# First products on x^T as loaded, normalised afterwards, in a hybrid short-convolution / RG-LRU layer

## The chip, the cores and the metric

The kernel runs on one core of one Trainium2 chip. The metric is device time in microseconds (us) of one execution. Names of engines in the profile: PE is TensorE (matmuls; PEld its weight loads), DVE is VectorE, ACT is ScalarE, POOL is GpSimd, SP is SyncE, which only issues DMAs.

## The reference

A decoder layer on x of 2048 positions by 1024 features, in float32. `DEPTH` is 1.

```python
xn = rms_norm(h, ln_g)                              # x / sqrt(mean(x^2) + eps) * ln_g
proj = jnp.einsum('bsd,de->bse', xn, w_in)          # 1024 -> 6 x 1024 columns
b_gate, c_gate, x_conv, g_conv, x_lru, g_lru = jnp.split(proj, splits, axis=-1)
y_conv = b_gate * causal_conv3(c_gate * x_conv)
y_conv = headwise_rms_norm(y_conv, 8, conv_out_g) * silu(g_conv)
u = causal_conv4(x_lru) + conv_b                    # then r, i from block-diagonal maps of u
a = exp(8 * r * log_sigmoid(lam)); drive = sqrt(1 - a^2) * (i * u)
h_t = a_t * h_{t-1} + drive_t                       # the scan
y_lru = headwise_rms_norm(h_t, 16, lru_out_g) * silu(g_lru)
out = rms_norm(h + concat(y_conv, y_lru) @ w_out, final_g)
```

The first line is what the change is about. The norm multiplies row s of x by one number, its root. In x^T (features on partitions, positions along the free axis) that is a factor for each column, and so it is in every product of a weight block with x^T: one can multiply first and scale the result's columns later.

## The kernel before, in words

**Products.** All arithmetic is on numbers of float32 width. A factor is split in two parts that TensorE takes (`fp32r`): a high part, made by a copy that rounds (`hi`, on ScalarE), and the rest (`low`, line 170, a subtraction on VectorE or POOL). A product of two split tiles is three matmuls of 128x128 by 128x512: high x high, high x low, low x high (`mm`, line 1023; "product" in this document means one such matmul). Tiles `th`/`tl` hold the parts of x^T (set `T[i, j]`, j of 4), `s` those of weights.

**Steps.** The positions are worked on in two halves of 1024, each in two blocks of 512. One step of the table `steps` (line 268) takes two groups of 128 output columns and both blocks of positions; the kinds are "l" (recurrent unit: its input and its gate), "a" and "b" (the convolution's C and x columns; B and gate). The features are halved too, so a step works on 2x2 blocks of weights and of x^T. From the fourth step on it uses a scheme of 7 block products (with sums of blocks, `s_plan`, line 192) in place of 8. The first three steps are plain: 96 products each, in four banks of PSUM called 11, 12, 21, 22: first digit the column group, second the block of positions. `prep` makes the next step's weight tiles while a step runs.

**Order of the work.** Each engine takes its instructions in the order in which the program writes them (`manual_schedule`, line 1067); nothing reorders them. Work after a bank is done is put off with `at(n, ...)`, line 144: it is written at the n-th `tick()` from there, and a tick comes ahead of every half bank of products in a plain step (line 1227). So the consumers `lru` (line 720), `conv_a` (834) and `conv_b` (870) write their parts among later steps: for "l" the bank copies, four convolution taps, tiles `st` (the split of u), the gate matmuls (line 764), sigmoids, tanh, exponential, root, scan. A gate matmul in TensorE's queue holds up all products behind it until its `st` tile is there.

**The opening.** SyncE loads the first four blocks of x as rows (512 KB each), weights of the first two steps and the next four blocks of x. `norm_rows` (line 527) squares a block on ScalarE, and VectorE scales it. `turn` (line 563) transposes four blocks to one x^T tile on TensorE (4 transposes of 128x128), and ScalarE or VectorE evicts it times `ln_g`. `first(j)` does that for the first block of 512 positions and `second(j)` for the second. `spin` writes transposes of the identity, which nobody reads, into TensorE's queue. The first step multiplies the first 512 positions (banks 11, 21), then the others (12, 22). The second step ("a") runs whole after it; `after1`/`after2` write the third step's weight split and the sums of x^T blocks (`bit`, line 1195) among the products.

## Time and profile before

| | |
|---|---|
| median of 3 runs | 1300.43 us (1299.43 to 1300.56) |
| the profiled execution | 1301.88 us, of which the span is 1300.0 us |
| granted TensorE clock | 0.998 |
| PE busy | 1284.9 us (99%) |
| DVE busy | 1030.9 us (79%) |
| ACT busy | 748.0 us (58%) |
| POOL busy | 207.2 us (16%) |
| DMA | 355.27 MB, mean 273 GB/s |

The page and the views behind it are of one execution. A row of a timeline gives the start in us from the span's begin, the duration, the engine, the line of the kernel, the operation, output and input tiles, sizes, how many instructions were merged, and in brackets the idle time ahead of it and what ended that. A line can be a helper's: L163 is every addition, subtraction and multiplication of two tensors. Where instructions follow each other closely, the start of the next is a better price than the duration, since durations of neighbours overlap by some 0.1 us.

### The profile page before, as it was taken

The numbers are of one execution on the slowest core, as the hardware profiler recorded it, in microseconds if no ns is written. First come the engines' busy times: TensorE is split into PE (matmuls) and PEld (weight loads), VectorE is DVE, ScalarE is ACT, GpSimd is POOL, SyncE is SP. The second block draws the span as 40 slices with busy tenths as digits, with TensorE's granted clock in tenths as the row PEclk, the third lists the DMA queues.
The fourth block names the chain that finished last, engine by engine and source line by source line (L and its number), as shares of the span: only waits on it lengthen the run. The fifth ranks groups of instructions, "written<-read, shape, count | busy, mean of one in ns | idle before, by whom it ended". The sixth has DMA issues, their size and how long they took to land.

```text
span 1300.0 us, 16684 instructions
## 1 busy us (share of the span) xinstructions
PE 1284.9 (99%) x5688; PEld 1059.0 (81%) x5688; DVE 1030.9 (79%) x1303; ACT 748.0 (58%) x1143; POOL 207.2 (16%) x173
## 2 busy tenths in 40 slices
PE   8999999999999999999999999999999999999997
PEld 6878888888888888888887888888888888887886
DVE  7799898999999988968656765677559777659886
ACT  8586857667565757666463636455466433445453
POOL 3102323332432320010010120101011000000000
PEclk9999999999999999999999999999999999999999
DMA  7138887898988888552899999999789897697654
GB/s 297 33 130 307 289 310 272 295 342 296 326 307 311 306 289 308 187 182 65 282 348 281 330 357 321 336 350 369 229 269 335 253 263 243 245 403 287 236 188 152
DMA packets 157956, 355.27 MB, mean 273 GB/s; under 512 B 16944, under 2 KB 51760, under 8 KB 157872
## 3 DMA queue, kind: packets, MB, share of 16 engines
q1 hardware_dynamic: 153264, 338.17, 75.6%
q0 software_dynamic: 4320, 15.73, 3.1%
q8 instruction: 45, 0.74, 0.2%
q10 hardware_dynamic: 288, 0.32, 0.1%
q14 instruction: 39, 0.32, 0.1%
HBM read 217.11 MB, written 137.04 MB: 272 GB/s over the span
## 4 chain that ended last, share of the span: by engine, by line
PE 88%; DVE 5%; DMA 4%; issue 1%; ACT 1%; POOL 0%; SPq 0%; DVEq 0%; POOLq 0%
PE bank L1028 86%; PE gate L764 2%; DVE s L163 1%; DMA s<-sd 1%; DMA tl<-td 1%; DMA xr<-od 1%; DMA s<-so 1%; DVE ob L163 0%; DVE raw L163 0%; DMA zr<-rsd 0%; DMA yd<-gl 0%; DVE tl L163 0%; ACT th L261 0%; POOL tl L163 0%; DVE x L551 0%
## 5 line engine op out<-in xcount | busy, mean ns | idle before, releaser
L1028 PE MATMUL bank<-th,s 128*128 128x512 f32 x3616 | 1121.7, 389 | 2.0 <-DMA s<-sd 0.7
L1028 PEld LDWEIGHTS bank<-th,s 128*128 128x128 f32 x3616 | 678.7, 188 | 145.5 <-ACT q L1364 1.9
L1028 PE MATMUL bank<-tl,s 128*128 128x512 f32 x1808 | 704.3, 390 | 0.5 <-POOL tl L163 0.2
L1028 PEld LDWEIGHTS bank<-tl,s 128*128 128x128 f32 x1808 | 339.4, 188 | 72.5 <-POOL tl L163 1.1
L163 POOL TENSOR_TENSOR s<-raw,s 128x512 fp32r<-128x512 f32 x62 | 114.0, 1852 | 283.9 <-ACT s L213 224.5
L213 ACT CAST s<-raw 128x512 fp32r<-128x512 f32 x140 | 84.5, 618 | 32.9 <-PE bank L1028 19.1
L163 DVE TENSOR_TENSOR s<-raw,s 128x512 fp32r<-128x512 f32 (+1 forms) x125 | 84.9, 702 | 10.2 <-ACT s L1091 6.5
L163 DVE TENSOR_TENSOR tl<-traw,th 128x512 fp32r<-128x512 f32 x85 | 58.3, 719 | 19.9 <-ACT th L451 10.0
L163 DVE TENSOR_TENSOR s<-s,s 128x512 fp32r<-128x512 f32 x105 | 73.0, 695 | 1.1 <-ACT s L213 1.1
L213 ACT CAST s<-s 128x512 fp32r<-128x512 f32 x105 | 65.0, 619 | 10.4 <-DVE s L163 10.4
L163 POOL TENSOR_TENSOR gb<-gb,sg 128x1024 f32<-128x1024 f32 x8 | 21.7, 2715 | 296.9 <-ACT sg L695 259.2
L736 DVE SCALAR_TENSOR_TENSOR u<-xl,pt,u 128x1024 f32<-128x1024 f32 x48 | 61.6, 1283 | 6.8 <-ACT u L732 6.2
L1364 ACT COPY q<-bank 128x512 f32<-128x512 f32 x58 | 33.8, 583 | 49.6 <-PE bank L1028 45.6
L848 DVE SCALAR_TENSOR_TENSOR t<-p,pt,t 128x1024 f32<-128x1024 f32 x32 | 46.5, 1453 | 15.0 <-ACT t L845 14.3
L163 DVE TENSOR_TENSOR st<-u,st 64x512 fp32r<-64x512 f32 x64 | 52.4, 818 | 2.0
L771 ACT ACTIVATE r<-gate,pt 64x512 f32<-64x512 f32 x64 | 43.7, 684 | 17.2 <-PE gate L764 16.4
L163 DVE TENSOR_TENSOR raw<-raw,zr 128x512 f32<-128x512 f32 x64 | 41.1, 682 | 8.7 <-DMA zr<-rsd 8.7
L1368 ACT COPY rr<-bank 128x512 f32<-128x512 f32 x31 | 18.1, 584 | 49.4 <-PE bank L1028 49.4
L771 ACT ACTIVATE i<-gate,pt 64x512 f32<-64x512 f32 x64 | 43.8, 684 | 1.1
L451 ACT CAST th<-traw 128x512 fp32r<-128x512 f32 x64 | 36.2, 618 | 13.3 <-DVE traw L163 10.7
L163 DVE TENSOR_TENSOR traw<-traw 128x512 f32<-128x512 f32 x60 | 41.7, 699 | 2.7 <-DMA traw<-in_w_out_dram 1.7
L1368 ACT COPY u<-bank 128x512 f32<-128x512 f32 x27 | 15.8, 585 | 47.7 <-PE bank L1028 47.1
(181 smaller groups left out, 1272.4 us busy)
## 6 DMA issues: line engine op xcount, KB each, us to landing
sd<-s SPq DMA_DIRECT2D x151, 512.0 KB
s<-sd SPq DMA_DIRECT2D x151, 512.0 KB
raw<-in_w_in_dram SPq DMA_DIRECT2D x104, 256.0 KB
raw<-yd SPq DMA_DIRECT2D x64, 256.0 KB
traw<-in_w_out_dram SPq DMA_DIRECT2D x64, 256.0 KB
so<-so SPq DMA_DIRECT2D x22, 512.0 KB
s<-so SPq DMA_DIRECT2D x22, 512.0 KB
yd<-gl SPq DMA_DIRECT2D x32, 256.0 KB
```

The costliest lines, as they stand in the source:

```text
L163: (eng or nc.vector).tensor_tensor(out=out, in0=a, in1=b, op=op)
L213: nc.scalar.copy(dst[i][0], val(i))
L451: nc.scalar.copy(self.dst[i, j][0], self.r[i, j])
L736: nc.vector.scalar_tensor_tensor(out=v["u"], in0=o1[:, 1 + j:1 + j + N2], scalar=lw[j], in1=v["u"], op0=ALU.mult, op1=ALU.add)
L764: nc.tensor.matmul(ps[j], v["gw"][n][:, j, :], v["st"][j][:, sl], start=(n == 0), stop=(n == 1))
L771: nc.scalar.activation(out=g_[hi, sl], in_=v["ps"][j][src], func=AF.Sigmoid, bias=pt[src, bias + k:bias + k + 1])
L848: nc.vector.scalar_tensor_tensor(out=tcur["t"], in0=p[:, 2 + j:2 + j + N2], scalar=cw[j], in1=tcur["t"], op0=ALU.mult, op1=ALU.add)
L1028: nc.tensor.matmul(bank, a[:, js], b, start=start and n == 0, stop=stop and n == 2, skip_group_check=more)
L1364: nc.scalar.copy(q1, bk["A"])
L1368: nc.scalar.copy(u2, bk["A"])
```

## The change: what it does

- x^T is loaded from a copy of x in DRAM that is stored by columns (`in_xt`, used before for later positions only): eight blocks of 128 features by 512 positions. They are scaled by `ln_g` and split (`raw_hi`, `raw_lo`), not normalised. `first` and its 32 transposes fall away.
- TensorE runs banks 11 and 21 of step one on them and then banks 11 and 21 of step two (`products`). Four banks hold raw results. Banks of step one are copied out (`RAW`), and one of step two; the other is read where it lies.
- The first 512 rows of x are loaded a second time as half rows (`xh`), squared on ScalarE and VectorE, summed, and rooted: one number per position. `roots` transposes it, spread over 128 columns, so that a tile `rr` has the roots along the free axis, the same on all partitions.
- The raw results are multiplied by `rr`. x^T, still in SBUF, is multiplied by `ln_g` and `rr` in one instruction per block (`scaled`, eight of them on VectorE), and split anew, eight casts on ScalarE and eight subtractions on POOL, for the third step and the sums.
- `second`, banks 12 and 22 of step one and then of step two follow. Step two has four ticks behind that point in place of eight, so what is put off by ticks moves: the first gate matmuls stand behind 228 products, where they stood behind 192. The sums of blocks (`bit`) are written two a tick. `klam` (a small constant) is made later. The recurrent unit's result of the first pair goes into tile `u`, not into `gl`.

The order on three engines. TensorE's first instructions (`tp` is a transpose's output, `x_152` to `x_155` the first four blocks of x). Before:

```order
L561 MATMUL spin<-ident 128x128 x28
L567 MATMUL tp<-ident,x_152 128x128
L561 MATMUL spin<-ident 128x128 x4
L567 MATMUL tp<-ident,x_153 128x128
L561 MATMUL spin<-ident 128x128 x4
L567 MATMUL tp<-ident,x_154 128x128
```

Now:

```order
L541 MATMUL spin<-ident 128x128 x34
L1152 MATMUL bank<-th,s 128x512 x4
L1152 MATMUL bank<-tl,s 128x512 x2
L1152 MATMUL bank<-th,s 128x512
L1152 MATMUL bank<-tl,s 128x512
```

The products come directly behind the spins; no transpose stands ahead of them. VectorE, at the last turned block of `second` and behind it (`rr` is the spread roots, `xl` and `gl` the copies of step one's raw banks). Before:

```order
L574 TENSOR_SCALAR traw<-tp,pt 128x512
L163 TENSOR_TENSOR tl<-traw,th 128x512
L163 TENSOR_TENSOR s<-raw,s 128x512 x2
L580 MEMSET rs_659 128x32
L163 TENSOR_TENSOR traw<-traw 128x512 x2
L736 SCALAR_TENSOR_TENSOR u<-xl,pt,u 128x1024 x2
```

Now:

```order
L552 TENSOR_SCALAR traw<-tp,pt 128x512
L162 TENSOR_TENSOR tl<-traw,th 128x512
L162 TENSOR_TENSOR xl<-xl,rr 128x512
L162 TENSOR_TENSOR gl<-gl,rr 128x512
L1207 SCALAR_TENSOR_TENSOR traw<-traw,pt,rr 128x512 x8
L558 MEMSET rs_704 128x32
L162 TENSOR_TENSOR traw<-traw 128x512 x2
L162 TENSOR_TENSOR s<-raw,s 128x512
L716 SCALAR_TENSOR_TENSOR u<-xl,pt,u 128x1024 x2
```

Ten instructions, two scalings of copies and eight of x^T, now stand ahead of the sums and the taps. POOL from its first weight split on. Before:

```order
L163 TENSOR_TENSOR s<-raw,s 128x512 x2
L163 TENSOR_TENSOR tl<-traw,th 128x512 x7
L724 MEMSET xl 128x4
L838 MEMSET p 128x2
L711 TENSOR_SCALAR bh<-bd 128x256
```

Now:

```order
L162 TENSOR_TENSOR s<-raw,s 128x512 x2
L162 TENSOR_TENSOR tl<-raw,th 128x512
L704 MEMSET xl 128x4
L162 TENSOR_TENSOR tl<-traw,th 128x512 x12
L825 MEMSET p 128x2
L691 TENSOR_SCALAR bh<-bd 128x256
```

Of the twelve low parts of x^T four are `second`'s and eight those of the scaled blocks; all twelve stand behind the opening.

The core of the diff:

```diff
-        for b in range(NB - 2):
-            norm_rows(b)()
...
+        def get_x(kt):
+            nc.sync.dma_start(tr[kt % NB][kt // NB * 2], xt[kt * P:(kt + 1) * P, 0:C])
...
+        for f, *v in ((get_w, 0, 0), (get_x, 0), (get_w, 0, 2), (get_x, 1), (get_x, 2), (get_x, 3),
+                      (get_w, 0, 1), (get_x, 4), (get_w, 0, 3), (get_x, 5), (get_x, 6), (get_x, 7),
+                      (get_w, 1, 0), (get_w, 1, 2), (get_w, 1, 1), (get_w, 1, 3)):
+            f(*v)
         for b in range(NB, 2 * NB):
             nc.sync.dma_start(x0[b], x[b * P:(b + 1) * P, :])
...
+        for b in range(NB):
+            for n in range(2):
+                nc.sync.dma_start(xh[b][n], x[b * P:(b + 1) * P, n * C:(n + 1) * C])
...
+        def raw_hi(kt, eng=None):
...
+                nc.scalar.activation(out=T[i, j][0], in_=tr[j][i // 2], func=AF.Copy, scale=gain(kt))
...
+        def raw_lo(kt):
+            i, j = kt // NB * 4, kt % NB
+            nc.vector.scalar_tensor_tensor(out=T[i, j][1], in0=tr[j][i // 2], scalar=gain(kt),
+                                           in1=T[i, j][0].bitcast(F32), op0=ALU.mult, op1=ALU.subtract)
...
+        raw = [[bank(), bank()] for _ in range(2)]
+        for part in range(2):
+            for j in range(NB):
+                products(0, raw[0], part, j, (0, 4), j == 0)
+        for b in range(NB, 2 * NB):
+            norm_rows(b)
+        lru0 = lru(0, 0)
+        lru0(11, raw[0][0], RAW)
+        lru0(21, raw[0][1], RAW)
...
+        for part in range(2):
+            for j in range(NB):
+                if part == 1 and j == 2:
+                    second(0)
+                products(1, raw[1], part, j, (0, 4))
...
+        tt(rs0, rs0, rest, ALU.add)
+        nc.scalar.activation(out=rs0, in_=rs0, func=AF.Sqrt, scale=1.0 / D, bias=eps)
+        nc.vector.reciprocal(out=rs0, in_=rs0)
+        conv0 = conv_a(0, 0)
+        conv0(21, raw[1][1], RAW)
+
+        def roots():
+            ps = pss.tile([P, C], F32, tag="s", name="rsb")
+            for b in range(NB):
+                nc.tensor.transpose(ps[:, b * P:(b + 1) * P], rs0[:, b:b + 1].broadcast_to((P, P)), ident)
+            rsb[0] = sm("rr")
+            nc.scalar.copy(rsb[0], ps)
+
+        def scaled(j):
+            for i in (0, 4):
+                v = tr[j][i // 2]
+                nc.vector.scalar_tensor_tensor(out=v, in0=v, scalar=gain(j + i), in1=rsb[0],
+                                               op0=ALU.mult, op1=ALU.mult)
+                Tp[j].hi(i)
+                Tp[j].lo(i, g)
...
             if j == 2:
...
+                roots()
+                lru0(11, None, rsb[0])
+                lru0(21, None, rsb[0])
+            if j >= 2:
+                scaled(2 * j - 4)
+                scaled(2 * j - 3)
...
+        for which, b in plain(1, (22, 12), after1):
+            kept[which] = b
+        conv0(12, kept[12], None)
+        conv0(21, None, rsb[0])
```

More of the change, by code (lines that the diff above doesn't have):

```diff
@@ L858, in put @@
             else:
-                xx[which] = aux("xx")
+                if which not in xx:
+                    xx[which] = aux("xx")
                 combine(xx[which], bank, other)
+                if other is RAW:
+                    return
             if which == 12:
@@ L1067, in hymba_kernel, with get_w @@
     with tc.manual_schedule(engines={ENG.PE, ENG.Activation, ENG.DVE, ENG.Pool, ENG.SP}):
-        spin(28)
-        make_klam()
-        Wr = [load_s(0)]
+        spin(34)
+        klam_late = make_klam()
+        Wr = [[piece("raw") for _ in range(4)] for _ in range(2)]
+        tr = [{} for _ in range(NB)]
+        raw0 = [wt("hl", "traw", bufs=HL) for _ in range(NB)]
+        for j in range(NB):
+            for i in range(2):
+                tr[j][2 * i] = raw0[j][:, i * C:(i + 1) * C]
+        def get_w(m, i):
+            half, q = divmod(i, 2)
+            nc.sync.dma_start(Wr[m][i], w_in[cols[steps[m][0]][half] + steps[m][2], q])
@@ L1095, in s_lo @@
         def s_lo(m, i, eng=None):
             low(Wr[m][i], Sp[m][i], eng)
-        tr = [{} for _ in range(NB)]
-        Tp = [TPrep(j, tr[j], T) for j in range(NB)]
-        raw0 = [wt("hl", "traw", bufs=HL) for _ in range(NB)]
-        def first(j):
-            for i in range(2):
-                tr[j][2 * i] = raw0[j][:, i * C:(i + 1) * C]
-                turn(0, j + i * NB, tr[j][2 * i], i, 0 if i or j else 4)
-        for i in range(3):
-            s_hi(0, i)
-        s_lo(0, 0, g)
-        s_lo(0, 2, g)
@@ L1112, in hymba_kernel @@
+        s_hi(0, 0, nc.vector)
+        raw_hi(0, nc.vector)
+        s_lo(0, 0)
+        s_hi(0, 2)
+        raw_lo(0)
+        s_lo(0, 2)
+        for kt in range(1, NB):
+            raw_hi(kt)
+            raw_lo(kt)
+        s_hi(0, 1)
         s_lo(0, 1)
-        Tp[0].hi(0)
+        raw_hi(4)
+        raw_lo(4)
         s_hi(0, 3)
-        Tp[0].hi(4)
-        Tp[0].lo(0)
-        s_lo(0, 3)
-        Tp[0].lo(4)
-        c11, c21 = bank(), bank()
-        def spread(order):
-            seen = []
-            for cc, i, w, t, v in order:
-                nc.tensor.matmul(cc, Sp[0][i][w][:, 0:P], T[t, 0][v], start=not any(b is cc for b in seen),
-                                 stop=False)
-                seen.append(cc)
@@ new lines, in hymba_kernel, with products @@
+        for kt in range(NB + 1, 2 * NB):
+            raw_hi(kt)
+            raw_lo(kt)
+        for i in (0, 2, 1, 3):
+            s_hi(1, i)
+            s_lo(1, i, g if i > 1 else None)
+        klam_late()
+        def products(m, cc, part, j, ts, spread=False):
+            a, b = ((cc[n], Sp[m][2 * n + part]) for n in range(2))
+            t = T[ts[part], j]
+            order = ((a, 0, 0), (b, 0, 0), (a, 1, 0), (b, 1, 0), (a, 0, 1), (b, 0, 1)) if spread else (
+                (a, 0, 0), (a, 0, 1), (a, 1, 0), (b, 0, 0), (b, 0, 1), (b, 1, 0))
+            for n, ((bk, s), w, v) in enumerate(order):
+                first = part == 0 and j == 0 and (n < 2 if spread else n % 3 == 0)
+                last = part == 1 and j == NB - 1 and n % 3 == 2
+                nc.tensor.matmul(bk, s[w][:, j * P:(j + 1) * P], t[v], start=first, stop=last,
+                                 skip_group_check=True)
```

176 lines of the change are left out of this document (67 added, 109 removed).

## The prediction

> **What bounds the kernel now.** I read the page first, for the engine that is full; then the windows by stage, for where the others are full too; then the timelines of the opening, because the change ends after the third step.
>
> ```profile
> span 1300.0 us, 16684 instructions
> PE 1284.9 (99%) x5688; PEld 1059.0 (81%) x5688; DVE 1030.9 (79%) x1303; ACT 748.0 (58%) x1143; POOL 207.2 (16%) x173
> ```
>
> TensorE sets the end: it is busy for 99%, and each microsecond by which its queue moves forward or back early stays to the last instruction. The profiled execution took 1301.88 us (1.88 outside the span); that is 1.45 above the median of 1300.43, so I work out a difference and put it on the median. The stages (columns: window, its length, then busy time and count of PE, PEld, DVE, ACT, POOL):
>
> ```profile
> 13.27:43.50 30.23, 29.29 (x144) 22.63 (x145) 21.26 (x28) 22.39 (x42) 9.82 (x9) 1.00 0.54 197
> 43.50:65.35 21.85, 21.85 (x99) 18.06 (x97) 17.52 (x25) 12.32 (x18) 1.77 (x3) 1.00 0.07 23
> 65.35:89.00 23.65, 23.65 (x105) 19.27 (x104) 21.51 (x32) 21.00 (x32) 0.10 (x1) 1.00 0.24 86
> 89.00:139.00 50.00, 49.33 (x217) 40.44 (x216) 48.04 (x55) 33.94 (x53) 13.94 (x10) 1.00 0.84 295
> ```
>
> From 89 to 139 us VectorE is busy for 48.0 of 50 us. It is nearly as full as TensorE, so TensorE cannot be brought forward by much unless VectorE is too. Before 65 us VectorE has some 20 us of idle time.
>
> **The opening, before and after.**
>
> ```profile
> 1.56 5.01 PE L561 MATMUL spin<-ident 128*128 128x128 f32 x28 [1.56 <-POOL ident masks.py:199]
> 8.37 0.33 PE L567 MATMUL tp<-ident,x 128*128 128x128 f32 x1 [1.79 <-DVE x L551]
> 13.27 2.24 PE L1124 MATMUL bank<-th,s 128*128 128x512 f32 x7 [0.41 <-ACT th L261]
> 16.68 1.03 PE L567 MATMUL tp<-ident,x 128*128 128x128 f32 x8
> 17.47 0.47 PE L1028 MATMUL bank<-th,s 128*128 128x512 f32 x1
> 65.35 0.39 PE L764 MATMUL gate<-st,bh 128*128 128x512 f32 x1
> 65.58 0.39 PE L764 MATMUL gate<-st,bl 128*128 128x512 f32 x1
> 4.96 1.06 ACT L539 ACTIVATE junk<-x 128x1024 f32<-128x1024 f32 x1 [0.24 <-DMA x<-in_x_dram]
> 10.00:20.00 10.00, 8.70 (x46) 6.31 (x47) 7.03 (x12) 9.34 (x18) 4.41 (x3) 1.00 1.04 399
> ```
>
> Today the first product runs at 13.27, after load, squares, scaling, transposes and split. The first gate matmul runs at 65.35, when the 192 products of two steps are done. A product costs 0.2275 us start to start (65.58 - 65.35), eight transposes 0.79 (17.47 - 16.68).
>
> In the changed kernel the first product needs one weight block, one block of x^T and their splits. The first 512 KB landed at 4.96 and the loads moved 399 GB/s (last column of the last row), so 256 KB blocks land from about 4.3 on, one each 0.65 us (an estimate from these two rows), always ahead of the six products (1.37 us) that each x^T block feeds. The 34 spins, at 5.01/28 = 0.179, end at 7.65, and by then the five VectorE instructions on the first blocks are about done (0.67 each at most, by a row further down). So products run from 7.65 without a wait: 84 of them take 19.1, to 26.75; eight transposes, to 27.55; twelve more products, to 30.3. **Gain so far** against the old order: about 10 us.
>
> Then a chain of short instructions ends last. ScalarE and VectorE need these prices:
>
> ```profile
> 37.80 0.69 ACT L572 ACTIVATE traw<-tp,pt 128x512 f32<-128x512 f32 x1 [0.80 <-PE tp L567]
> 39.07 0.62 ACT L1159 CAST th<-traw 128x512 fp32r<-128x512 f32 x1 [0.58 <-DVE traw L574]
> 9.08 0.62 ACT L536 ACTIVATE junk<-x 128x512 f32<-128x512 f32 x1
> 9.60 0.19 ACT L536 ACTIVATION_READ_ACCUMULATOR junk<-x 128x1 f32 x1
> 34.56 0.74 DVE L574 TENSOR_SCALAR traw<-tp,pt 128x512 f32<-128x512 f32 x1
> ```
>
> Behind the first turned blocks (27.55) ScalarE has an eviction and two casts (to 29.3), then four half-row squares at 0.72 (to 32.1); VectorE has its own four, with a POOL subtraction beside them, to 33.3. Root and reciprocal end at 34.15, and only behind them in VectorE's queue stands the eviction of the second turned block (34.9), then cast (35.5), low part (36.2), POOL's low part (37.45). TensorE waits there with five of twelve products, goes on to 39.3, turns the last block and spreads the roots, to 40.5. The remaining products of both steps, 72 at 0.2275, would end at 56.9 against 65.35: a lead of 8.4 us. The spread roots lie in SBUF at 42.35, after the eviction, two casts and one copy.
>
> **What VectorE must do from 42.35 to the first gate matmul.** By the program the gates now stand behind 228 products, not 192; in the old run that amount of TensorE work is done at 65.35 + 36 x 0.2275 = 73.5. Ahead of the `st` tiles that the gates need, VectorE has: 24 operations of 128x512 on two tensors (two scalings of copied banks, two of kept ones among them), the 8 new L1207 instructions that scale x^T, 3 convolution taps of 1024, one 1024 multiplication and 2 `st` instructions. Their prices, start to start:
>
> ```profile
> 58.36 0.69 DVE L163 TENSOR_TENSOR tl<-traw,th 128x512 fp32r<-128x512 f32 x1
> 58.96 0.69 DVE L163 TENSOR_TENSOR u<-traw 128x512 f32<-128x512 f32 x1
> 252.73 0.74 DVE L604 SCALAR_TENSOR_TENSOR xcol<-xcol,pt 128x512 f32<-128x512 f32 x1
> 253.40 1.28 DVE L848 SCALAR_TENSOR_TENSOR t<-p,pt,t 128x1024 f32<-128x1024 f32 x1
> 47.35 2.60 DVE L736 SCALAR_TENSOR_TENSOR u<-xl,pt,u 128x1024 f32<-128x1024 f32 x2
> 60.77 1.22 DVE L163 TENSOR_TENSOR gl<-gl,sg 128x1024 f32<-128x1024 f32 x1
> 63.35 2.84 DVE L163 TENSOR_TENSOR st<-u,st 64x512 fp32r<-64x512 f32 x4
> ```
>
> 24 x 0.60 + 8 x 0.67 + 3 x 1.22 + 1.13 + 2 x 0.72 = 26.0 us (0.67 is 253.40 - 252.73, the L604 instruction being of the same form). Nothing in that list waits for a product that is done later than that. Alone it would end at 68.4, 5.1 before 73.5.
>
> **The cost that decides: POOL beside VectorE.** The change puts eight POOL subtractions (the low parts of the scaled x^T) beside the eight L1207 and what follows. Here is what such neighbours do today:
>
> ```profile
> 36.55 1.27 POOL L163 TENSOR_TENSOR tl<-traw,th 128x512 fp32r<-128x512 f32 x1 [2.46 <-ACT th L261]
> 37.03 1.34 DVE L163 TENSOR_TENSOR s<-raw,s 128x512 fp32r<-128x512 f32 x1 [0.35 <-ACT s L1091]
> 96.71 1.54 POOL L163 TENSOR_TENSOR s<-raw,s 128x512 fp32r<-128x512 f32 x1 [20.45 <-ACT s L213]
> 97.28 2.06 DVE L677 SCALAR_TENSOR_TENSOR gl<-r,pt,gl 128x1024 f32<-128x1024 f32 x1
> 112.78 3.70 POOL L163 TENSOR_TENSOR s<-raw,s 128x512 fp32r<-128x512 f32 x2 [6.27 <-DMA yd<-gb]
> 111.08 2.56 DVE L736 SCALAR_TENSOR_TENSOR u<-xl,pt,u 128x1024 f32<-128x1024 f32 x2
> 113.55 1.78 DVE L163 TENSOR_TENSOR s<-raw 128x512 f32<-128x512 f32 x1
> 115.37 1.67 DVE L163 TENSOR_TENSOR s<-s,raw 128x512 f32<-128x512 f32 x1
> ```
>
> The VectorE instruction at 37.03 takes 1.34 instead of 0.69 and ends 0.55 after POOL's does: it stood still while POOL worked. The taps at 111.08 ran at full speed although POOL had started at 112.78; POOL waited, and then the two at 113.55 and 115.37 took 3.45 in place of 1.38. The two engines take turns, and where VectorE is full a POOL subtraction costs it (3.45 - 1.38)/2 = 1.04 us. Bounds: nothing (POOL always waits) and POOL's whole 1.27. I take 1.04. Eight cost 8.3, the last subtraction of the third turned block 0.65 (1.34 - 0.69), the gate weights' split about 0.85 (estimate: one subtraction of half the size). Together 9.8.
>
> The first `st` pair is then ready at 42.35 + 26.0 + 9.8 = 78.15, and the gates run 4.7 us later than today, in place of 8.4 earlier. Behind the waiting gates stand all products of the third step. What is late next: ScalarE's copies of weight blocks for that step, which stand behind the eight casts of scaled x^T, so TensorE halts at its start too; these halts lie ahead of the gates and are not added. After the gates VectorE's queue, full until 139, has no more in it than before but for the scan, its copy and the multiplication behind it, 3.6 us that now stand later. The least room there is between the low part that ends at 119.4 and its product:
>
> ```profile
> 92.76 0.50 PE L1028 MATMUL bank<-th,s 128*128 128x512 f32 x1 [0.68 <-ACT q L1364]
> 118.75 0.68 DVE L163 TENSOR_TENSOR s<-s,s 128x512 fp32r<-128x512 f32 x1
> ```
>
> That product runs 132 products after 92.76, near 123; the room of 3.6 us is just used up. I add nothing.
>
> Small parts: 28 transposes fewer are in the times above. The klam instructions move from ahead of the first scaling to where VectorE waits for turned blocks:
>
> ```profile
> 3.25 0.17 DVE L122 TENSOR_SCALAR kl<-kl 128x8 f32<-128x8 f32 x1 [0.27 <-ACT kl L120]
> 7.29 0.17 DVE L138 TENSOR_SCALAR klam<-kl 128x8 f32<-128x8 f32 x1
> ```
>
> Those 4 us are costed at nothing there. SyncE's queue reads 2.1 MB more; at 0.65 us for 256 KB the half rows land by 25, before their squares at 29. If they were late, each microsecond would move the 42.35.
>
> **Sum:** + 4.7 us, so 1301.88 + 4.7 = 1306.6 for an execution like the profiled one, and **1305.2 us** on the median.
>
> **Rivals.**
>
> A, POOL yields. VectorE's queue is back to back, so it may win the turn each time, as the taps at 111.08 did; POOL's low parts are needed only from the third bank of the third step on. The gates are at 68.4 plus the little that is left, and the least room in VectorE's later queue limits the lead to 4 to 5 us: **1296 us**. It decides where a POOL subtraction costs VectorE under (5.1 - 0.65 - 0.85)/8 = 0.45 us. For it: the taps. Against it: the pairs at 37.03, 97.28 and 113.55. The Trainium skill speaks for it in part: "SBUF — State Buffer", section "Who interferes with whom", says that the engine which issues first holds the shared port pair for its whole instruction and that issue order decides who blocks; the rows show both orders, and by turns.
>
> B, VectorE does not matter and the whole lead of 8.4 stays: **1292 us**. Against it: 48.04 busy of 50 us from 89 on.
>
> C, the strided columns of x^T drag the opening loads to half their rate. The half rows then land near 41 and the roots end some 8 us later, and with them all behind: **1313 us**. The weights, in rows of the same 2 KB, were part of the 399 GB/s, so I give it little.
>
> D, the costs meet in the middle (about 0.45 us for each subtraction) and the move does nothing: **1300 us**.
>
> **Chances.** Forecast 0.52 (its own range 1303 to 1308: the subtraction at 1.27, the opening late by 1), A 0.22, B 0.06, C 0.08, D 0.12. A measurement of this kernel can tell 0.2%, 2.6 us. Faster: A and B, 0.28. Within: D and the lower edge of the forecast, 0.14. Slower: 0.58. The range takes in A and ends above the forecast's upper bound: 1295.5 to 1309.5; B and C are left out.
>
> **What would show it.** In the changed profile: first product at about 7.7; L1207 instructions of about 1.7 to 1.9 us each in place of 0.74, with POOL subtractions between them; TensorE idle before the first gate matmuls, released by `st`, which start near 78; VectorE without idle time from 42 to 139. The forecast is wrong if the L1207 take 0.7 (A), if the gates start before 73, or if TensorE's first halves run with gaps that a DMA ends (C).

## The result, and the profile after

The changed kernel takes **1315.78 us** (median of 4, 1314.51 to 1316.63) against 1300.49 of the old one on the same chip: a ratio of 1.0117, 95% interval 1.0099 to 1.0134. It is 15.3 us slower; the forecast was 4.7 slower.

From the page of the profile:

```profile
span 1314.6 us, 16650 instructions
PE 1286.9 (98%) x5654; PEld 1058.6 (81%) x5654; DVE 1045.1 (79%) x1314; ACT 747.6 (57%) x1140; POOL 219.0 (17%) x179
```

The same four stages as before (window, its length, then busy time and count of PE, PEld, DVE, ACT, POOL; then the granted clock):

```profile
13.27:43.50 30.23, 29.36 (x145) 23.90 (x145) 22.24 (x54) 20.23 (x43) 8.49 (x8) 1.00 0.78 302
43.50:65.35 21.85, 17.64 (x76) 13.62 (x74) 21.66 (x21) 12.31 (x19) 13.84 (x9) 1.00 0.00 1
65.35:89.00 23.65, 15.77 (x50) 11.97 (x50) 22.75 (x33) 8.93 (x15) 1.87 (x4) 0.78 0.00 0
89.00:139.00 50.00, 46.03 (x192) 36.53 (x193) 44.74 (x54) 39.48 (x59) 9.77 (x8) 0.97 0.71 251
```

TensorE was busy for all of 43.5 to 89 us in the old kernel; now it is idle for 12 of 45.5 us there, and VectorE is busy for 44.4 of them. From 65 to 89 the granted clock is 0.78 on average. Nearly the whole loss lies ahead of 113 us (13.9 of the 14.6 us between the two profiled spans, worked out below). These are TensorE's halts from 57 us on (its timeline; in brackets the idle time and what ended it); behind the last one it never waits again within 60 us:

```profile
58.88 0.50 PE L1018 MATMUL bank<-th,s 128*128 128x512 f32 x1 [1.51 <-ACT s L1098]
60.48 0.73 PE L1018 MATMUL bank<-th,s 128*128 128x512 f32 x2 [0.87 <-DVE s L162]
66.02 0.94 PE L1018 MATMUL bank<-th,s 128*128 128x512 f32 x2 [2.49 <-DVE s L162]
78.57 0.76 PE L744 MATMUL gate<-st,bh 128*128 128x512 f32 x1 [5.67 <-DVE st L162]
90.11 0.69 PE L744 MATMUL gate<-st,bh 128*128 128x512 f32 x1 [2.67 <-DVE raw L162]
91.52 0.80 PE L744 MATMUL gate<-st,bh 128*128 128x512 f32 x1 [0.28 <-ACT i L751]
105.70 0.50 PE L1018 MATMUL bank<-th,s 128*128 128x512 f32 x1 [1.56 <-ACT q L1399]
112.46 0.50 PE L1018 MATMUL bank<-th,s 128*128 128x512 f32 x1 [1.01 <-ACT rr L1403]
```

Together 16.1 us. In the old kernel there is one halt in that stretch, the 0.68 at 92.76 that the prediction shows. The opening went as forecast: first product at 6.87, the first turned blocks at 26.93, the spread roots in SBUF at 42.86 (forecast 7.65, 26.75, 42.35). VectorE's timeline from there, and ScalarE's copy of the bank that ended the last halt:

```profile
42.86 1.39 DVE L162 TENSOR_TENSOR xl<-xl,rr 128x512 f32<-128x512 f32 x1 [0.32 <-ACT rr L1202]
44.78 10.58 DVE L1207 SCALAR_TENSOR_TENSOR traw<-traw,pt,rr 128x512 f32<-128x512 f32 x8
55.32 3.42 DVE L162 TENSOR_TENSOR traw<-traw 128x512 f32<-128x512 f32 x2
77.74 2.84 DVE L162 TENSOR_TENSOR st<-u,st 64x512 fp32r<-64x512 f32 x4
111.83 0.57 ACT L1403 COPY rr<-bank 128x512 f32<-128x512 f32 x1
```

The `st` instructions start at 77.74 in place of 63.35, which the prediction had nearly right (first pair ready at 78.15; the gates ran at 78.57). Against the equal-work point of 73.5 that is 5.1 us late, forecast 4.7. The other 10 us or so come behind the gates. The copy `rr` at 111.83 is the place up to which things are late. In the old kernel it stands at

```profile
96.54 0.58 ACT L1368 COPY rr<-bank 128x512 f32<-128x512 f32 x1
```

so it is 15.3 us later now, as is the median (the two profiled spans differ by 14.6).

How the lateness gets there is on ScalarE's timeline: a cast that VectorE releases, and the copy `q`, now and in the old kernel.

```profile
87.64 0.62 ACT L1240 CAST th<-traw 128x512 fp32r<-128x512 f32 x1 [2.69 <-DVE traw L162]
105.08 0.57 ACT L1399 COPY q<-bank 128x512 f32<-128x512 f32 x1
```

```profile
78.66 0.62 ACT L1200 CAST th<-traw 128x512 fp32r<-128x512 f32 x1 [0.83 <-DVE traw L163]
92.12 0.58 ACT L1364 COPY q<-bank 128x512 f32<-128x512 f32 x1 [0.25 <-PE bank L1028]
```

In the changed kernel VectorE's timeline shows no wait from 42.86 up to the work that releases this cast, and ScalarE's none from the cast to `rr`. VectorE brings the cast 9.0 us late, and from it to `rr` ScalarE takes 24.2 us in place of 17.9. Neither waits for TensorE on that way. In the old kernel `q` does: there TensorE, without a halt from 41.63 on, sets the time up to `q`.

### The profile page after: what moved, and what is told of

The parts are those of the page before. It is cut to its first block, busy times and chain, and to the rows that moved or that the text cites. A ratio compares the mean times of both kernels' runs of the same rounds, so it can differ in the third digit from the quotient of the medians.

```text
span 1314.6 us, 16650 instructions
## 1 busy us (share of the span) xinstructions
PE 1286.9 (98%) x5654; PEld 1058.6 (81%) x5654; DVE 1045.1 (79%) x1314; ACT 747.6 (57%) x1140; POOL 219.0 (17%) x179
## 4 chain that ended last, share of the span: by engine, by line
PE 86%; DVE 3%; ACT 2%; DMA 2%; issue 1%; SPq 0%; DVEq 0%; ACTq 0%
PE bank L1018 84%; PE gate L744 2%; DMA tl<-td 1%; DVE s L162 1%; DMA yd<-gl 1%; ACT s L212 0%; ACT th L1297 0%; DVE ob L162 0%; DMA s<-sd 0%; DVE raw L162 0%; DMA yd<-gb 0%; ACT r L751 0%; DVE t L835 0%; DVE sums L645 0%; DVE r L778 0%
## 5 line engine op out<-in xcount | busy, mean ns | idle before, releaser
L1018 PE MATMUL bank<-th,s 128*128 128x512 f32 x3560 | 1108.0, 390 | 9.7 <-DVE s L162 3.4
L1018 PEld LDWEIGHTS bank<-th,s 128*128 128x128 f32 x3560 | 670.0, 188 | 154.1 <-DVE s L162 4.2
L1018 PE MATMUL bank<-tl,s 128*128 128x512 f32 x1780 | 694.3, 390 | 0.4 <-DVE tl L162 0.2
L1018 PEld LDWEIGHTS bank<-tl,s 128*128 128x128 f32 x1780 | 335.2, 188 | 70.4 <-POOL tl L162 0.6
L162 DVE TENSOR_TENSOR tl<-traw,th 128x512 fp32r<-128x512 f32 x80 | 54.1, 712 | 18.2 <-ACT th L450 14.2
L835 DVE SCALAR_TENSOR_TENSOR t<-p,pt,t 128x1024 f32<-128x1024 f32 x32 | 46.5, 1452 | 13.4 <-ACT t L832 12.6
L1409 ACT COPY u<-bank 128x512 f32<-128x512 f32 x31 | 18.1, 585 | 47.2 <-PE bank L1018 47.2
L1403 ACT COPY u<-bank 128x512 f32<-128x512 f32 x27 | 15.8, 585 | 50.0 <-PE bank L1018 48.7
```

The lines of the kernel that those rows point to most:

```text
L162: (eng or nc.vector).tensor_tensor(out=out, in0=a, in1=b, op=op)
L835: nc.vector.scalar_tensor_tensor(out=tcur["t"], in0=p[:, 2 + j:2 + j + N2], scalar=cw[j], in1=tcur["t"], op0=ALU.mult, op1=ALU.add)
L1018: nc.tensor.matmul(bank, a[:, js], b, start=start and n == 0, stop=stop and n == 2, skip_group_check=more)
L1403: nc.scalar.copy(u2, bk["A"])
L1409: nc.scalar.copy(rr, bk["A"])
```

## The experiments

Three theories were held against each other at first. **V**: VectorE's queue, and behind it ScalarE's, is late, and TensorE only meets that lateness again and again. **K**: TensorE loses time of its own, since its clock halves behind each halt. **G**: the gates stand too early in TensorE's queue.

### TensorE kept at work in its halts

```diff
         def after2(s):
+            spin({0: 8, 1: 13}.get(s, 0))
...
+            if h == 0 and k == 0:
+                spin((36, 20)[i])
             for j in range(2):
                 ps.append(pss.tile([P, C], F32, tag="s", name="gate"))
```

> The changed kernel, with transposes of the identity that nobody reads written into TensorE's queue at the four places where it stood idle and came back at half the granted clock (8 and 13 ahead of the first two half banks of the third step, 36 and 20 ahead of the first and the second gate matmuls; 0.163 us each, less than the idle time there). Theory V (VectorE's queue, and behind it ScalarE's, is late and TensorE only meets it again and again): the clock stays up, TensorE arrives earlier and waits longer, and the time stays at 1315.8, within 1. Theory K (the half-speed stretches behind the halts, 58.88 to 103.98 us holding 6.7 us more than products and halts account for, of which some 4 lie behind the first gates, are part of the loss): 1311 to 1312.

Measured: 1315.4 us, ratio 1.0105 (1.0090 to 1.0120), so K's 1311 to 1312 did not come. The granted clock in windows (window, length, TensorE's busy time and count, clock), of the changed kernel:

```profile
67.00:69.00 2.00, 2.00 (x6) 0.50 0.00 0
```

and of this one:

```profile
67.00:69.00 2.00, 2.00 (x9) 1.00 0.00 0
79.00:81.00 2.00, 2.00 (x6) 0.50 0.00 0
```

TensorE's timeline here:

```profile
72.09 4.09 PE L541 MATMUL spin<-ident 128*128 128x128 f32 x36
78.50 0.77 PE L746 MATMUL gate<-st,bh 128*128 128x512 f32 x1 [2.31 <-DVE st L162]
90.04 0.50 PE L746 MATMUL gate<-st,bh 128*128 128x512 f32 x1 [1.22 <-DVE raw L162]
112.37 0.51 PE L1020 MATMUL bank<-th,s 128*128 128x512 f32 x1 [1.03 <-ACT rr L1406]
```

The slow stretch at 67 is gone (9 matmuls in two us in place of 6); those behind the first and the second gates stayed, for 2.31 and 1.22 us of idle time were left ahead of them. The 77 extra transposes took some 9 us in all (the 36 took 4.09, 0.114 each), less than I had reckoned. Yet gates, second gates and the last halt stand within 0.1 us of where they stood. TensorE has that much time to give away. The clock's loss is real and hidden: K falls for the stretch at 67. The other slow stretches this run does not test; that they cost nothing in the changed kernel follows from the timelines in the section on the result, in which neither VectorE nor ScalarE waits for TensorE up to `rr`.

### Without POOL's eight subtractions

```diff
-                Tp[j].hi(i)
-                Tp[j].lo(i, g)
+                hi = tp_.tile([P, C], F32R, tag=f"th{home[i]}{j}", name="th")
+                nc.scalar.copy(hi, v)
+                T[i, j] = hi, T[i, j][1]
```

> The changed kernel without POOL's eight subtractions for the scaled x^T: the low parts of the unscaled blocks stay in their place, so the products of the third step and some later ones are computed from wrong low parts. Everything else runs. It prices POOL's turns: by the rows of the changed kernel VectorE loses 10.58 - 8 x 0.67 = 5.2 us on the eight scalings, 2.0 on the two sums behind them and 0.9 on the next low part, 8.1 together. Theory V: VectorE is 8.1 us earlier for good and so is the end: 1307.5 (1306 to 1309). Theory K: the first gates are reached without a halt, and with the halt goes the slow clock: some 1301 to 1303. My prediction's price of 1.04 us for each, with nothing added behind the gates, would be 8.3 less.

Measured: 1309.13 us, ratio 1.0060 (1.0043 to 1.0077), at the upper edge of V's range. VectorE's timeline:

```profile
44.82 5.38 DVE L1207 SCALAR_TENSOR_TENSOR traw<-traw,pt,rr 128x512 f32<-128x512 f32 x8
50.16 1.38 DVE L162 TENSOR_TENSOR traw<-traw 128x512 f32<-128x512 f32 x2
53.70 0.69 DVE L162 TENSOR_TENSOR s<-raw,s 128x512 fp32r<-128x512 f32 x1 [2.17 <-ACT s L1098]
71.70 2.84 DVE L162 TENSOR_TENSOR st<-u,st 64x512 fp32r<-64x512 f32 x4
```

POOL's turns cost what was forecast: 10.58 - 5.38 = 5.2 us on the eight scalings, 3.42 - 1.38 = 2.0 on the two sums and 0.9 on the next low part, 1.0 us for each POOL subtraction (forecast 1.04). The Trainium skill, "SBUF — State Buffer", section "Who interferes with whom", says that a VectorE instruction with two SBUF inputs contends with a GpSimd instruction that reads SBUF, and calls the port pair that they share an exclusive lock. The eight with and without POOL beside them (10.58 and 5.38 us) agree that they contend. Of the 8.1 us VectorE then waits 2.17 for ScalarE, so `st` starts 6.04 earlier, and every later mark moves by as much. TensorE still halts 6.21 us at the first gates and 2.23 at the second, at half clock behind both. K's 1301 to 1303 did not come, but K had them from gates that are reached without a halt, and they were not: what the clock costs behind them this run does not test.

### Gates later

```diff
-                for slots, *fs in ((5 - early, sth), (6 - early, stl), (8, lambda: gates(0)), (8, lambda: sigs(0)),
-                                   (10, lambda: gates(1)), (11 - h - early, lambda: sigs(1)), (12, s1, s0),
+                q = h == 0 and k == 0
+                for slots, *fs in ((5 - early, sth), (6 - early, stl), (10 if q else 8, lambda: gates(0)),
+                                   (10 if q else 8, lambda: sigs(0)), (11 if q else 10, lambda: gates(1)),
+                                   (11 if q else 11 - h - early, lambda: sigs(1)), (12, s1, s0),
```

> The changed kernel with the first unit's gates moved back: the first pair of gate matmuls and their sigmoids two ticks later (behind 252 products in place of 228), the second pair one tick later. Theory V: VectorE's queue is the same, TensorE passes the place at 78 us without a halt but waits elsewhere for the same VectorE and ScalarE work: 1315.8, within 1.5. Theory G (TensorE loses because the gates stand too early in its queue, and the products behind them could have gone ahead): the 5.1 us at the first gates come back, 1310 to 1312.

Measured: 1317.20 us, ratio 1.0119 (1.0104 to 1.0134). The products went ahead, and TensorE then stood still in one piece (its timeline):

```profile
94.40 0.79 PE L744 MATMUL gate<-st,bh 128*128 128x512 f32 x1 [11.33 <-ACT i L751]
```

G falls: the wait moves, it isn't made by the place of the gates.

### The low parts on VectorE

```diff
                 Tp[j].hi(i)
-                Tp[j].lo(i, g)
+                Tp[j].lo(i)
```

> The changed kernel with the eight low parts of the scaled x^T on VectorE in place of POOL. Theory V: VectorE pays 8 x 0.60 = 4.8 us in place of the 8.1 that POOL's turns take from it, so the end is 3.3 us earlier: 1312.5 (1311 to 1314). If POOL's subtractions cost VectorE little (the rival in which POOL yields), VectorE would only gain work: up to 1320.6. Theory K: 3.3 us and a part of the half-speed stretches, 1309 to 1311.

Measured: 1319.31 us, ratio 1.0133 (1.0118 to 1.0148), slower still. Not POOL's price was wrong but mine for the move: each low part needs ScalarE's cast of the block that VectorE has just scaled, and VectorE waits for it, eight times, as its timeline shows:

```profile
44.85 0.74 DVE L1207 SCALAR_TENSOR_TENSOR traw<-traw,pt,rr 128x512 f32<-128x512 f32 x1
46.28 0.69 DVE L162 TENSOR_TENSOR tl<-traw,th 128x512 fp32r<-128x512 f32 x1 [0.69 <-ACT th L260]
81.38 2.84 DVE L162 TENSOR_TENSOR st<-u,st 64x512 fp32r<-64x512 f32 x4
```

With each low part written one block late (`lag` holds it), the wait has cover:

```diff
-                Tp[j].lo(i, g)
+                if lag:
+                    lag.pop()()
+                lag.append(lambda j=j, i=i: Tp[j].lo(i))
+            if j == NB - 1:
+                lag.pop()()
...
+        lag = []
```

> The changed kernel with the eight low parts of the scaled x^T on VectorE, each written one block late, so that ScalarE's cast is done when VectorE comes to it (with the low part right behind its block VectorE waited 0.69 us eight times). Theory V (what VectorE has to do from 42 us on sets the end): 8 x (0.67 + 0.60) = 10.2 us in place of 13.5 with POOL's turns, so up to 3.3 earlier, less what VectorE then waits for ScalarE's cast of a weight block (2.17 in the run without low parts): 1313.5 (1312 to 1315). If VectorE's waits for ScalarE can't be hidden: 1319, as with the low part right behind.

Measured: 1313.32 us, ratio 1.0089 (1.0072 to 1.0106), as V has it, though the interval overlaps that of the changed kernel; the trace is clearer, with `st` at 74.90, 2.84 earlier. A full VectorE does such a subtraction itself for 0.60 us; given to POOL it cost it 1.0.

### The unit's sigmoids earlier

ScalarE is never idle from 87.6 to 112.4 us, and eight sigmoids stand there that stood ahead of 78 in the old kernel. So theory V was refined to **VS**: VectorE 9 us late at 87, ScalarE 6 more.

```diff
-                for slots, *fs in ((5 - early, sth), (6 - early, stl), (8, lambda: gates(0)), (8, lambda: sigs(0)),
-                                   (10, lambda: gates(1)), (11 - h - early, lambda: sigs(1)), (12, s1, s0),
...
+                f = h == 0 and k == 0
+                for slots, *fs in ((5 - early, sth), (6 - early, stl), (7 if f else 8, lambda: gates(0)),
+                                   (7 if f else 8, lambda: sigs(0)), (8 if f else 10, lambda: gates(1)),
+                                   (9 if f else 11 - h - early, lambda: sigs(1)), (12 - 0 * f, s1, s0),
...
```

> The changed kernel with the first unit's gates and sigmoids written earlier: gates and sigmoids of the first pair one tick earlier, the second pair's gates and sigmoids two ticks earlier. ScalarE's eight sigmoids (8 x 0.69 = 5.5 us) then lie in its idle time behind the first gates (5.63 and 2.69 us, up to 87.6), not in the stretch 87.6 to 112.4, in which it is never idle. Theory VS (VectorE is 9 us late at 87, and ScalarE, with the unit's work now among the copies of the next steps, adds 6 by 112): 5.5 less, 1310.3 (1309 to 1312). Theory V (VectorE's lateness is all of it): 1315.8, within 1. By the logic of my prediction (gates hold the products behind them, so gates 12 products earlier cost 2.7): 1318.5.

Measured: 1314.84 us, ratio 1.0103 (1.0088 to 1.0118). VS fails here: no 5.5 us. The order did what it should (the first sigmoid at 84.56, not 88.69), but the second four now stand ahead of casts that VectorE needs, and VectorE waits in its turn (its timeline):

```profile
95.50 0.69 DVE L162 TENSOR_TENSOR tl<-traw,th 128x512 fp32r<-128x512 f32 x1 [2.06 <-ACT th L1300]
```

The copy `rr` came at 111.50, 34.06 us behind the start of `st`, the same as in the changed kernel (34.09). The chain of waits behind this run ends in other links, a weight DMA among them; which of them would have come next was not settled.

### Without any scaling

```diff
-            for i in (0, 4):
-                v = tr[j][i // 2]
-                nc.vector.scalar_tensor_tensor(out=v, in0=v, scalar=gain(j + i), in1=rsb[0],
-                                               op0=ALU.mult, op1=ALU.mult)
-                Tp[j].hi(i)
-                Tp[j].lo(i, g)
+            pass
...
-            tt(dst, dst if bank is None else bank, other, ALU.mult)
+            if bank is not None:
+                nc.scalar.copy(dst, bank)
```

> The changed kernel without all scaling by the roots: the eight scalings of x^T with their casts and low parts are left out (the products of the third step and later ones use the unscaled blocks), and so are the four multiplications of the raw results (one is a plain copy on ScalarE). The opening, its lead of 8 us, the roots and the four ticks stay. Theory VS: VectorE is 2.5 us earlier than in the old kernel, but ScalarE's unit work still stands 3 ticks later among the copies, 6.3 us more between the same two casts: TensorE gives its lead back there, 1302 (1300 to 1304). Theory V (VectorE alone): 1297.5 (1296.5 to 1299). If neither matters the lead stays: 1292.

Measured: 1305.14 us, ratio 1.0028 (1.0018 to 1.0037), outside all three expectations: VS, the nearest, ends at 1304, and its premise that VectorE is 2.5 us earlier failed, since `st` comes 3.9 later. Even with all the new work left out, the rest of the change is 3.9 us slower than the old kernel. The timelines of VectorE and ScalarE:

```profile
50.57 0.69 DVE L162 TENSOR_TENSOR s<-raw,s 128x512 fp32r<-128x512 f32 x1 [4.83 <-ACT s L1099]
67.25 2.84 DVE L162 TENSOR_TENSOR st<-u,st 64x512 fp32r<-64x512 f32 x4
47.30 0.59 ACT L811 COPY gl<-bank 128x512 f32<-128x512 f32 x1 [3.72 <-PE bank L1019]
101.34 0.58 ACT L1399 COPY rr<-bank 128x512 f32<-128x512 f32 x1
```

In the old kernel the same copy of bank 22 stood at

```profile
43.78 0.59 ACT L827 COPY gl<-bank 128x512 f32<-128x512 f32 x1 [2.08 <-PE bank L1028]
```

Here is something that I had not seen at all. TensorE is ahead by its count of products, but it runs the second step's first banks before the first step's second banks. So the unit's input is complete 3.5 us **later** than in the old kernel, and VectorE waits 4.83 for a cast that stands behind the two copies. In the changed kernel this is covered by the scalings.

### The old kernel with VectorE's and POOL's new work alone

```diff
+        for j in range(NB):
+            for i in range(2):
+                kt = j + i * NB
+                sc, lw_ = (tp_.tile([P, C], F32, tag=f"{q}2{j}", name="extra") for q in ("th", "tl"))
+                nc.vector.scalar_tensor_tensor(out=sc, in0=tr[j][2 * i], scalar=pt[:, LN_G + kt:LN_G + kt + 1],
+                                               in1=tr[j][1], op0=ALU.mult, op1=ALU.mult)
+                tt(lw_, sc, tr[j][3], ALU.subtract, g)
         put(22, c22, None)
```

> The old kernel with VectorE's and POOL's new work alone: behind its last turned block eight more instructions of the form of the scaling on VectorE, each with a POOL subtraction behind it, written to tiles that are free then and that nobody reads. VectorE gets 13.5 us by the changed kernel's rows (5.4 of its own, 8.1 of POOL's turns); its idle time there was 3.28, later 2.19 and 1.70. Theories V and VS: 13.5 - 3.3 - 2.2 - 1.7 = 6.3 us later, 1307 (1305 to 1309). If VectorE's room takes it: under 1302. If such work costs its whole length: 1314.

Measured: 1314.18 us, ratio 1.0097 (1.0082 to 1.0112), 13.0 us slower, nearly the whole length of the added work. (That came to 14.4 us, 42.56 to 56.93, because each tile was used twice and VectorE waited for POOL to have read it, 8.7 us of the 14.4.) My 6.3 took VectorE's idle time for room. Only the first 3 us were; the waits of 2.19 and 1.70 came again, just later, on its timeline:

```profile
69.75 0.69 DVE L163 TENSOR_TENSOR s<-raw,s 128x512 fp32r<-128x512 f32 x1 [2.19 <-ACT s L1091]
75.94 2.84 DVE L163 TENSOR_TENSOR st<-u,st 64x512 fp32r<-64x512 f32 x4
86.02 2.60 DVE L848 SCALAR_TENSOR_TENSOR t<-p,pt,t 128x1024 f32<-128x1024 f32 x2 [1.70 <-ACT t L845]
```

They are round trips: VectorE waits for a ScalarE instruction that itself stands behind VectorE's work.

The 13.0 us are not VectorE's alone, though. The timelines of TensorE and ScalarE:

```profile
76.78 0.77 PE L764 MATMUL gate<-st,bh 128*128 128x512 f32 x1 [10.76 <-DVE st L163]
105.48 0.59 ACT L1371 COPY q<-bank 128x512 f32<-128x512 f32 x1 [1.01 <-PE bank L1028]
106.12 0.50 PE L1028 MATMUL bank<-th,s 128*128 128x512 f32 x1 [0.68 <-ACT q L1371]
```

The first gates run 11.4 us later than the 65.35 of the old kernel. From there to the product behind `q` TensorE has no halt, as in the old kernel, but it takes 29.3 us in place of 27.4 (92.76 - 65.35): its granted clock was 0.50 from 77 to 81 us. Here `q` waits for TensorE, so these 1.9 us count. K, which the changed kernel hides, holds here for that much.

### The old kernel with less for VectorE

```diff
-            nc.vector.scalar_tensor_tensor(out=v["u"], in0=o1[:, 1 + j:1 + j + N2], scalar=lw[j],
-                                           in1=v["u"], op0=ALU.mult, op1=ALU.add)
+            if h or k or j == 3:
+                nc.vector.scalar_tensor_tensor(out=v["u"], in0=o1[:, 1 + j:1 + j + N2], scalar=lw[j],
+                                               in1=v["u"], op0=ALU.mult, op1=ALU.add)
```

> The old kernel without two of the first unit's taps on VectorE (2.60 us ahead of the st instructions; the unit's first input is then incomplete). If VectorE's time at st alone set the end there too, it would come 2.6 earlier: 1298. If TensorE, which has no idle time from 41.6 to 92 us in the old kernel, and VectorE are two bounds of the same length there, of which the later one counts: 1300.5, within 1; then work added to VectorE costs its length (as the eight extra instructions did) and work taken from it brings nothing.

Measured: 1300.71 us, ratio 1.0000 (0.9991 to 1.0010). `st` starts at 61.01, 2.34 earlier, and the copy `rr` stays at 96.33. In the old kernel two bounds of nearly the same length meet at the gates: TensorE's and VectorE's. In the changed kernel the first gate ran 0.83 us behind the start of `st`; by that VectorE would have allowed it at 64.2 in the old one, and TensorE came at 65.35. The later one counts.

### From `st` to 112 us

By now the start of `st` told the time. Two runs took work away behind it, one on each engine.

```diff
-            nc.vector.scalar_tensor_tensor(out=tcur["t"], in0=p[:, 2 + j:2 + j + N2], scalar=cw[j],
-                                           in1=tcur["t"], op0=ALU.mult, op1=ALU.add)
+            if h or k:
+                nc.vector.scalar_tensor_tensor(out=tcur["t"], in0=p[:, 2 + j:2 + j + N2], scalar=cw[j],
+                                               in1=tcur["t"], op0=ALU.mult, op1=ALU.add)
```

> The changed kernel without the first convolution's two taps on VectorE (2.60 us for both, right behind the st instructions; this convolution's result is then wrong). So far the end lies as much later than in the old kernel as VectorE's first st instruction does (63.35 there), within 1 us in eight kernels. Theory S (from st on VectorE and ScalarE pass their queues on without room until 112 us, VectorE first): 2.5 less, 1313.3. If ScalarE or the deferred order carries the time from st on: 1315.8, within 1.

```diff
-            nc.scalar.activation(out=v["r"], in_=v["r"], func=AF.Exp, scale=klam[:, k:k + 1])
+            nc.scalar.activation(out=v["r"], in_=v["r"], func=AF.Exp if h or k else AF.Tanh, scale=klam[:, k:k + 1])
...
-            nc.scalar.activation(out=v["T"], in_=v["T"], func=AF.Sqrt)
+            nc.scalar.activation(out=v["T"], in_=v["T"], func=AF.Sqrt if h or k else AF.Tanh)
```

> The changed kernel with tanh in place of the first unit's exponential and root (the unit's first result is then wrong), so that ScalarE loads no table at 102.7, 106.2 and 108.5 us: 3 x 1.28 = 3.8 us less in the stretch in which it is never idle. Theory S: TensorE's last two halts, 1.56 and 1.01 on copies of banks, go with it, and no more than they: 1313.2. If VectorE's queue carries the time there too: 1315.8, within 1.

Measured: 1312.72 us (ratio 1.0083, 1.0068 to 1.0098) without the taps, 1313.08 us (1.0086, 1.0071 to 1.0101) without the table loads. In the profiles the copy `rr` moved from 111.83 to 109.48 and 108.73. Both engines carry the time there, one behind the other. Without the taps `rr` comes 2.35 us earlier. Without ScalarE's 3.8 us it comes 3.1 earlier; then `q` waits for TensorE's bank (1.01 us). TensorE's last halt is gone, and half of the one before (its timeline, without table loads):

```profile
105.43 0.50 PE L1018 MATMUL bank<-th,s 128*128 128x512 f32 x1 [0.68 <-ACT q L1399]
```

### A kernel built on the finding

The old kernel with only the first 48 products on unscaled columns; x^T for everything else comes from transposes of normalised rows, the second block first. Its core on TensorE:

```diff
+        for b in (4, 5, 6, 7, 0, 1, 2, 3):
             nc.sync.dma_start(x0[b], x[b * P:(b + 1) * P, :])
...
             if j == 2:
+                roots()
                 put = lru(0, 0, 1, 1)
+                put(11, c11, rsb[0])
+                put(21, c21, rsb[0])
...
-        for which, b in plain(1, (11, 12, 22, 21), after1):
+        for which, b in plain(1, (22, 12, 11, 21), after1):
```

> A different kernel, built on theory S: the old one with only its first 48 products on the columns of x^T as loaded. The second block of rows is loaded, normalised and turned next, then the first, by transposes as in the old kernel, so that x^T is not scaled on VectorE and no new low parts fall to POOL; only the two raw banks are multiplied by the spread roots. Step two keeps its eight ticks and runs the second block's banks first. VectorE gets eight low parts of 0.67 us before 16 us, where it has room, and 2 x 0.60 later. The second block's rows land some 5 us earlier than they are needed today. Theory S: the st instructions start 3 to 5 us earlier than at 63.35, and the end with them: 1296 to 1298. If VectorE has no room before st after all: 1300, within 1.5, or above.

Measured: 1315.69 us, ratio 1.0106 (1.0090 to 1.0123). My hope of an `st` 3 to 5 us earlier was wrong; that a late `st` makes a late end held: VectorE reached `st` only at 77.29. Squares of rows and the `klam` instructions (50.09 to 54.24) now stood in its full stretch, and POOL beside it. At first the rows set the pace, then VectorE (timelines of TensorE and VectorE):

```profile
20.52 0.33 PE L554 MATMUL tp<-ident,x 128*128 128x128 f32 x1 [1.59 <-DVE x L540]
24.88 2.33 DVE L530 SCALAR_TENSOR_TENSOR traw<-x 128x1024 f32<-128x1024 f32 x1
77.29 2.84 DVE L164 TENSOR_TENSOR st<-u,st 64x512 fp32r<-64x512 f32 x4
```

Here, too, TensorE carries the time behind the gates: they run at 78.12, 12.8 us later than in the old kernel, and from there to the product behind `q`, without a halt, 1.5 us more are lost at half clock.

None of the kernels beat the old one.

### All runs in one table

Start of VectorE's first `st` and of ScalarE's copy `rr` from the timelines; "later" is the median less that of the old kernel on the same chip.

| kernel | `st` starts | `rr` copy | between | `st` later than 63.35 | time later |
|---|---|---|---|---|---|
| old | 63.35 | 96.54 | 33.2 | | |
| old, two taps less | 61.01 | 96.33 | 35.3 | -2.3 | -0.6 |
| no scaling at all | 67.25 | 101.34 | 34.1 | 3.9 | 3.9 |
| no POOL low parts | 71.70 | 105.79 | 34.1 | 8.4 | 7.5 |
| low parts on VectorE, one block late | 74.90 | 109.67 | 34.8 | 11.6 | 12.1 |
| old, eight scalings more | 75.94 | 109.89 | 34.0 | 12.6 | 13.0 |
| columns for 48 products only | 77.29 | 110.79 | 33.5 | 13.9 | 13.9 |
| gates later | 77.37 | 113.50 | 36.1 | 14.0 | 15.5 |
| sigmoids earlier | 77.44 | 111.50 | 34.1 | 14.1 | 13.6 |
| TensorE kept at work | 77.67 | 111.74 | 34.1 | 14.3 | 13.7 |
| **the change** | 77.74 | 111.83 | 34.1 | 14.4 | 15.3 |
| no table loads | 77.75 | 108.73 | 31.0 | 14.4 | 11.3 |
| no convolution taps | 77.90 | 109.48 | 31.6 | 14.6 | 11.0 |
| low parts on VectorE at once | 81.38 | 116.63 | 35.3 | 18.0 | 17.6 |

Where no work is taken away behind `st`, the time is later by what `st` is later, to within 1.5 us, over a range from 3.9 to 18 (a median is known to some 2 us). In the one run with `st` earlier than 63.35 it brings nothing.

The table is a rule for these kernels, not one chain of waits. In the changed kernel the way from `st` to `rr` leads through VectorE and then ScalarE. In the old kernel, and in the two that keep the eight ticks of its second step (eight scalings more; columns for 48 products only), TensorE carries it from the gates to `q`. That the ways are equally long, 33.2 and 34.1 us, is luck. So is a part of the agreement in those two: their gates are 11.4 and 12.8 us late, and the slow clock adds 1.9 and 1.5.

## Why the prediction was wrong, step by step

**Opening: right.** Load, spins, 84 products, transposes and roots came within 0.8 us of the walk, with some luck: the first product came 0.8 sooner, and the 84 products took 20.1 us in place of 19.1. The loads kept their rate (398 GB/s from 10 to 20 us, where the old kernel had 399), so rival C has no part in it; that its 1313 lies near the measured time is luck.

**The list on VectorE and POOL's price: right.** The forecast was 26.0 + 9.8 us and the first pair of `st` at 78.15; the first gate matmul ran at 78.57. POOL's subtractions cost 8.1 in place of 8.3. The form in which it would show was off: L1207 at 1.32 us each, not 1.7 to 1.9, since some three of POOL's eight turns (2.9 of 8.1 us) fell on the instructions behind. Rival A (POOL yields) would need 0.67 there.

**The comparison: wrong.** Before the gates the forecast came true in its own terms: TensorE was 5.1 us late there, against 4.7. But I set 78.15 against 73.5, the moment at which TensorE has done 228 products in the old run, because the gates now stand behind 36 products more. That credits the change with 8.2 us of TensorE's work done ahead of the gates. The experiment with extra transposes shows that TensorE's time has no value in this stretch of the changed kernel: it can spend 9 us of it on nothing. By the table, what counts is when VectorE comes to `st`, against when it did: 78.15 less 64.8 (63.35 + 2 x 0.72), 13.4 us, and 1313.8 for the median by the prediction's own numbers.

**"After the gates ... I add nothing": the term that failed, put at 0 and measured at some 10 us.** From the stage view I had read that VectorE is full from 89 to 139 us, and then looked for its room in one low part near 119. The queue had no room ahead of that: of its idle time before 65 us (17.6 us, not some 20) only waits of 3.28 and 2.19 lay between 42.35 and `st`. And I did not look at ScalarE's queue behind the gates at all. The runs showed both in its place. VectorE brings ScalarE's cast at 87.64, 9.0 us late; from there to `rr` ScalarE needs 6.3 us more than before, 5.5 of them (8 x 0.69) for eight sigmoids that stood ahead of that cast in the old kernel. 9.0 + 6.3 = 15.3. Without the convolution's taps on VectorE `rr` came 2.35 us earlier, without ScalarE's table loads 3.1. What stays open is why moving the sigmoids alone won nothing: another chain, with waits of VectorE and a weight DMA, was as long.

TensorE only meets that lateness. It was 5.1 us late at the first gates and halted again at the second gates (2.67 and 0.28), at `q` (1.56, old 0.68) and at `rr` (1.01). Between the first gates and `q` it lost 7.9 us (105.70 - 92.76 = 12.9, less 5.1); 3.8 of them are those halts, and the 4 that are left are, by the windows at 0.50, the slow clock. 5.1 + 2.95 + 0.88 + 4 + 1.01 = 13.9; the two spans differ by 14.6. What sets the sum is the chain, not its parts; a shorter one is made up for by another, as the first experiment shows.

**"Halts at the third step's start lie ahead of the gates and are not added": right.** They were 4.87 us and a stretch at half clock, and taking that stretch away changed nothing.

**The clock: missing.** Nowhere did the prediction ask what TensorE's clock does behind a halt. In the changed kernel it cost nothing, because VectorE and ScalarE were later still. In the old kernel with eight scalings more it cost 1.9 us.

**Rival B** (the whole lead stays) was the furthest off. The run without any scaling shows that even the lead of 8.4 us was none for VectorE: the order of the banks gave it the unit's input 3.5 us later.

## What to carry to other kernels

Compare each engine's queue with its own old times, not with the engine that is busiest: where a second queue is full, work put into it can cost nearly its whole length at the end, and here an early start of the first engine paid for none of it. Follow the lateness on through every queue behind the place where you stop adding, ScalarE's too, before you put that term at nothing. Idle time of a full queue that waits for a round trip through another engine is no room; ask whether the releaser itself stands behind that queue. A reordering that is ahead in the count of products can still be behind for the one bank that the next engine waits for.

## What the runs showed of the hardware

TensorE's granted clock fell to half behind halts, and a product then took 0.43 us start to start in place of 0.2275 (changed kernel, TensorE's timeline behind the second gates):

```profile
92.54 0.63 PE L1018 MATMUL bank<-th,s 128*128 128x512 f32 x1
92.97 0.63 PE L1018 MATMUL bank<-tl,s 128*128 128x512 f32 x1
```

The granted clock of that window:

```profile
91.00:93.00 2.00, 1.72 (x5) 0.50 0.35 137
```

It took 3 to 5 us of work to come back. In the changed kernel the halts that were followed by it lasted 2.49, 5.67 and 2.67 us; one of 1.56 was not, nor were two of 1.51 and 0.87 with 0.7 us of work between them. In three other runs (gates later, no convolution taps, no table loads) two such halts were followed by it. The Trainium skill, "TensorE: Matmul & The Clock Gate", section "Part 1: The HAM clock gate", has the clock at half after an idle window of about 3.4 us and back after about as much work. The half and the way back agree; here halts of 2.5 us were enough, and the measurement decides.

The second finding is the price of POOL beside a full VectorE: 1.0 us for each subtraction (8.1 us for eight), more than the 0.60 that VectorE needs to do it itself.
